# Fourier mixing on one core: where a map quarter's arithmetic and the middle row's products stand

## The chip, the core and the metric

The kernel runs on one core of a Trainium2 chip. Six things work beside each other in that core: TensorE (PE in the rows, with its weight loads as PEld), VectorE (DVE), ScalarE (ACT), GpSimd (POOL), SyncE (SP, which issues most transfers) and the DMA engines. Each engine runs its own instructions in the order in which they stand, and waits where one needs what another engine has not finished. The metric is the device time of one execution in microseconds (us); less is better. The kernel was timed three times, and one execution was profiled.

## What is computed

The program is a trunk of two layers over 512 tokens of width 1024, in float32. The first layer mixes by a state-space scan and neighbourhood attention. The second one, which the change touches, mixes by a two-dimensional Fourier transform and a linear map. Each layer ends in a squared-ReLU MLP.

```python
def fourier_mix(h, w_f):
    hf = jnp.fft.fft2(h.astype(jnp.float32), axes=(1, 2), norm='ortho').real
    return hf.astype(h.dtype) @ w_f
...
        else:
            o = layer // 2
            out_l = fourier_mix(hl, w_fourier[o])
...
        h = h + g1[:, None, :] * rms_norm(out_l, norm_g[layer, 1])
        hf = modulate(rms_norm(h, norm_g[layer, 2]), sh2, sc2)
        h = h + g2[:, None, :] * rms_norm(sqrelu_mlp(hf, w_ff1[layer], w_ff2[layer]), norm_g[layer, 3])
```

## The kernel before

A float32 product is made of three fast ones. An operand is split into a rounded part `hi` (a cast on ACT) and the rest `lo` (a subtraction on DVE): `split_to` (L185). `mm3` (L106 to L108) then multiplies hi by hi, hi by lo and lo by hi. So each operand that is computed on the way costs ACT and DVE work before PE can use it.

The Fourier layer goes in these steps.

* **Stage 1** (L1147) transforms along the tokens and leaves its sums in PSUM tiles `pst`, which are then copied to `xh`, `xl` and `p2`.
* **Features** (the loop over `m_`, L1204 to L1215): for each of four blocks PE makes two products `pa` (L1199 and L1201, plain float32), one 258 and one 256 columns wide. Both are split into `abh` and `abl` (L185), and one column goes to `nyc` (L1210). One more product, `pn`, is split into the small operand `ny`.
* **The map** (`mapw(q)`, L1073) comes in four quarters of 256 output columns. Quarter q is loaded as one tile of 128x2048. On it DVE makes a difference `ws` of its halves (L1081), GpSimd clears a row of `ws`, DVE makes their sum in place (L1084), and both are split: two casts of 128x1024 on ACT and two subtractions of 128x1024 on DVE. A row of 256 elements (`wmid`) is loaded as `w5` and becomes the small operand `wn` (`stack3`, L1060). Quarter 0 (`w0`) is made much earlier, beside the MLP of the layer before. The raw tiles are `wraw82` (quarter 0), the second part of `td` (1), `wraw83` (2) and `w3` (3); the operands of quarters 1 to 3 are `whi44`/`wlo44`, `whi45`/`wlo45` and `whi46`/`wlo46`.
* **The last row** (`last_row(q)`, L1221): four DVE instructions (L1230 once, L1228 three times) that need the sum of quarter q and all four `nyc` columns, and write a quarter of `gn`.
* **Stage 3** (`stage3(q, j)`, L1240): for quarter q and half j of the features PE makes `pq` (12 products), which ACT copies to `qs` (L1256), and `pp` (12 products and one with `ny` and `wn`, L1250). DVE writes their difference to tile 2j of the result `oa` (L1259) and their sum to tile 2j+1 (L1260). For j = 0 there is the middle row: two products into `p2`, of `ny` with `wn` (L1263) and of a column of ones with `gn` (L1264, plain float32), which ACT copies into row 0 of tile 1 (L1265). Before the change this stands at the end of `stage3(q, 0)`.
* **What follows:** when the four quarters of j = 0 are done, tiles 0 and 1 of `oa` go through `residual` (a square with row sums on ACT at L176, `ms` at L178, the root on GpSimd at L180, two DVE passes at L858 and L859) and `normed` (another square over the new `h`, `ms`, a root, one pass `m` at L869). Then `to_cols` transposes both tiles on PE (`ptn`, L888) and splits them into the operand `f1fh`/`f1fl` of the second MLP, whose first products are `pf`. The tiles 2 and 3, from j = 1, follow in the same way.

The order on each engine isn't written out. The program is handed to a scheduler, which lays the instructions out along a modelled timeline; `behind(...)` (L188) tells it to place the instructions inside it only after the ones named. The result is one fixed order for each engine.

Of the kernel before, what the change touches and what calls it, by code (L numbers as in the profile page):

```python
# [93 lines left out]
def trunk(tc, I, out, dump=None):  # L94
# [15 lines left out]
    with es:  # L110
# [24 lines left out]
        def big(tag, dt, nm, n=4096):  # L135
            return bigp.tile([128, n], dt, tag=tag, name=nm)
# [739 lines left out]
        def halves_(t):  # L876
            return [t[:, c * 2052:c * 2052 + 2048] for c in range(2)]
# [172 lines left out]
        def tables():  # L1050
            SY.dma_start(alt, I["alt"])
            SY.dma_start(rev, I["rev"])
            P.memset(zero, 0.0)
            fo["m"] = big("fh", F32, "mf", 4104)
            fo["S"] = W.raw(I["tabS"].rearrange("(k p) n -> p k n", p=128), 4, 514)
            mapw(0, [t.rearrange("p (k n) -> p k n", k=8) for t in halves_(big("fl", F32R, "w0", 4104))])

        wq, plus = {}, {}

# [10 lines left out]
                V.tensor_tensor(f[r:r + 1, 0:n], src, rh.bitcast(F32), SUB)  # L1070
            A.copy(o, f[0:65, 0:n])

        def mapw(q, pair=None, t=None):  # L1073

            cols = slice(q * 256, q * 256 + 256)
            t = W.raw(None, 8, 256) if t is None else t.rearrange("p (k n) -> p k n", k=8)
            wr, wv = t[:, 0:4], t[:, 4:8]
            SY.dma_start(t, I["map"][q].rearrange("p (k n) -> p k n", k=8))
            hi, lo = pair or W.slot(8, 256)
            ws = wide("ws").rearrange("p (k n) -> p k n", k=4)  # L1080
            V.tensor_tensor(ws, wr, wv, SUB)  # L1081
            P.memset(ws[0:1, 0], 0.0)
            split_to(hi[:, 4:8], lo[:, 4:8], ws)
            V.tensor_tensor(wr, wr, wv, ADD)  # L1084
            split_to(hi[:, 0:4], lo[:, 0:4], wr)
            plus[q] = wr
            w5 = small_tile(F32, "w5")[0:1, 0:256]
            SY.dma_start(w5, I["wmid"][:, cols])
            wn = rw.tile([65, 256], F32R, tag="wn", name="wn", bufs=4)
            stack3(w5, wn, (0, 64), (32,))  # L1090
            wq[q] = hi, lo, wn
# [96 lines left out]
        for i in range(2):  # L1188
            evicted = A.copy(PS_[i][:, :, 0:256], ps4[2 + i].rearrange("p (e n) -> p e n", e=2))

        with behind(first, evicted):
            mapw(1, None, spare[:, 2052:4100])
        nyc = rw.tile([128, 4], F32, name="nyc")

        def feat(dst, X, e0, c0, n, row):
# [8 lines left out]
        for m_ in range(4):  # L1204
            ah, al = act_tile("ab")
            even, c = m_ < 2, (m_ % 2) * 128
            pa = ps_mm("pa")[:, 0:258]
            feat(pa, PE_, 0 if even else 2, c if even else 258 + c, 128, even)
            split_to(ah[:, 0:258], al[:, 0:258], pa)
            V.tensor_copy(nyc[:, m_:m_ + 1], pa[:, 0:1])  # L1210
            pa = ps_mm("pa")[:, 0:256]
            feat(pa, PS_, 2 if even else 0, (770 if even else 514) + c, 128, False)
            split_to(ah[:, 258:514], al[:, 258:514], pa)
            AB.append((ah, al))
        pn = ps_mm("pn")[0:1, 0:258]  # L1215
        feat(pn, PE_, 0, 256, 1, True)
        ny = rw.tile([65, 258], F32R, name="ny")
        stack3(pn, ny, (0, 32), (64,))
        mapw(2)
        mapw(3, None, big("fh", F32, "w3", 4104)[:, 0:2048])  # L1220
        gn = wide("gn")  # L1221

        def last_row(q):
# [5 lines left out]
                else:  # L1229
                    V.tensor_scalar(gn[:, cols], plus[q][:, 0], nyc[:, 0:1], None, MULT)  # L1230

        for q in range(4):
            last_row(q)
        SY.dma_start(h[:, 0], hd[0:128])
        SY.dma_start(h[:, 2], hd[128:256])
        for t in range(2):
# [4 lines left out]
        def stage3(q, j):  # L1241
            hi, lo, wn = wq[q]
            cols = slice(q * 256, q * 256 + 256)
            ka = slice(2 + j * 128, 130 + j * 128)
            kb = slice(258 + j * 128, 386 + j * 128)

            def cospart(dst, ks):
                for m_ in range(4):
                    mm3(dst, AB[m_][0][:, ks], AB[m_][1][:, ks], hi[:, m_], lo[:, m_], m_ == 0, False)
                T.matmul(dst, ny[:, ks], wn, start=False, stop=True)  # L1250

            pq = ps_mm("pq")
            for m_ in range(4):
                mm3(pq[:, 0:256], AB[m_][0][:, kb], AB[m_][1][:, kb], hi[:, 4 + m_], lo[:, 4 + m_], m_ == 0, m_ == 3)
            qs = wkp.tile([128, 260], F32, tag="z", name="qs", bufs=3)[:, 0:256]
            A.copy(qs, pq[:, 0:256])  # L1256
            pp = ps_mm("pp")
            cospart(pp[:, 0:256], ka)
            V.scalar_tensor_tensor(oa[:, 2 * j, cols], qs, -1.0, pp[:, 0:256], MULT, ADD)  # L1259
            V.tensor_tensor(oa[:, 2 * j + 1, cols], qs, pp[:, 0:256], ADD)  # L1260
            if j == 0:
                p2 = ps_mm("p2")[0:2, 0:256]
                T.matmul(p2, ny[:, 0:2], wq[q][2], start=True, stop=False)  # L1263
                T.matmul(p2, ones[:, 0:2], gn[:, cols], start=False, stop=True)  # L1264
                A.copy(oa[0:1, 1, cols], p2[0:1])  # L1265

        fh, fl = (halves(big(t, F32R, "f1" + t, 4104)) for t in ("fh", "fl"))
        ns, w1 = {}, {}
        left = [4, 4]
        for q, j in [(0, 0), (1, 0), (2, 0), (3, 0), (0, 1), (1, 1), (2, 1), (3, 1)]:  # L1270
            stage3(q, j)
            left[j] -= 1
            if j == 0 and left[0] == 0:
                for t in range(2):
# [153 lines left out]
```

## Time and profile before

| | |
|---|---|
| three timed runs | 1208.49, 1202.07, 1206.25 us, median 1206.25 |
| the profiled execution | 1203.99 us, of which 1202.2 us are its span (first to last instruction) |
| busy in the span | PE 1153.0 us (96%), DVE 764.3 (64%), ACT 496.9 (41%), POOL 88.4 (7%) |
| granted TensorE clock, mean | 0.985 of full |

The profile shows one execution. Times in its rows count from the start of the span. The Fourier layer's features and stage 3 lie between 782 and 826 us, and the MLP of the second layer from there to the end. Busy shares over the whole span say little of this stretch: PE is the engine that is nearly always busy, but here it is also the one that waits, so the rows below are of this stretch.

### The profile page before, as it was taken

The page shows a single profiled execution, that of the slowest core. Times are in us where ns is not written, and L with a number is a line of the kernel's source. Part 1 is how long each engine was busy: PE and PEld are TensorE (multiplying, and loading weights), DVE is VectorE, ACT ScalarE, POOL GpSimd, SP SyncE. Part 2 cuts the span into 40 slices and gives each one's busy share as a digit, 9 for nine tenths or more (in the row PEclk, how much of TensorE's full clock was granted, in tenths as well). Part 3 has the DMA queues.
Part 4 walks back from the last instruction along what each step waited for, and adds up shares of the span by engine and source line. Part 5 has one row for each costly group of instructions (what it writes and reads, how often), then busy time and mean ns, then how long its engine had stood idle before and what let it go on. Part 6 is the DMA issues. An engine that isn't in the chain of part 4 may idle for free. (4 is left out here: it accounts for less than half of the span.)

```text
span 1202.2 us, 15748 instructions
## 1 busy us (share of the span) xinstructions
PE 1153.0 (96%) x6330; PEld 943.7 (78%) x6330; DVE 764.3 (64%) x1130; ACT 496.9 (41%) x821; POOL 88.4 (7%) x134
## 2 busy tenths in 40 slices
PE   4999999989999999999999999988999999999997
PEld 2687888778977988888888887767988888888886
DVE  7658999666558667667666447787664344344345
ACT  6665446358626643323223133357543223323322
POOL 1001332200002000000000000203000000000001
PEclk8998999989999999999999999998999999999999
DMA  7617444543257375455465422442362332332201
GB/s 269 229 42 209 103 111 132 173 160 102 84 196 261 109 245 194 163 203 180 170 210 168 147 86 72 133 181 77 135 240 76 105 105 71 105 105 75 101 1 71
DMA packets 42368, 168.28 MB, mean 140 GB/s; under 512 B 12587, under 2 KB 14128, under 8 KB 30006
## 3 DMA queue, kind: packets, MB, share of 16 engines
q1 hardware_dynamic: 38726, 155.11, 37.1%
q0 software_dynamic: 2560, 10.42, 3.9%
q10 hardware_dynamic: 1008, 1.72, 0.4%
q8 instruction: 50, 0.82, 0.3%
q14 instruction: 24, 0.20, 0.1%
HBM read 160.49 MB, written 6.75 MB: 139 GB/s over the span
## 5 line engine op out<-in xcount | busy, mean ns | idle before, releaser
L66 ACT CAST whi<-wraw 128x2048 fp32r<-128x2048 f32 (+2 forms) x103 | 147.8, 1459 | 294.0 <-PE pff L108 175.3
L70 DVE TENSOR_TENSOR wlo<-wraw,whi 128x2048 fp32r<-128x2048 f32 (+2 forms) x81 | 161.3, 2000 | 120.5 <-ACT whi L66 120.2
L106 PE MATMUL pff<-whi,ah 128*128 128x512 f32 (+1 forms) x482 | 189.2, 394 | 0.0
L108 PE MATMUL pff<-whi,al 128*128 128x512 f32 (+1 forms) x482 | 189.2, 393 | 0.0
L107 PE MATMUL pff<-wlo,ah 128*128 128x512 f32 (+1 forms) x482 | 188.9, 393 | 0.0
L1000 DVE TENSOR_TENSOR facc<-facc,pff 128x512 f32<-128x512 f32 (+1 forms) x113 | 76.6, 680 | 96.2 <-PE pff L108 96.1
L209 DVE SCALAR_TENSOR_TENSOR gacc<-wraw,cs,gacc 128x1024 f32<-128x1024 f32 x76 | 97.3, 1281 | 24.2 <-DMA wraw<-w_mod 20.8
L107 PE MATMUL pf<-f1fl,whi 128*128 128x512 f32 (+1 forms) x288 | 106.6, 373 | 2.1 <-DVE f1fl L185 1.2
L106 PE MATMUL pf<-f1fh,whi 128*128 128x512 f32 (+1 forms) x288 | 105.7, 374 | 1.9 <-ACT f1fh L185 1.6
L106 PEld LDWEIGHTS pff<-whi,ah 128*128 128x128 f32 x482 | 90.5, 188 | 21.5 <-DVE facc L1000 0.4
L108 PEld LDWEIGHTS pff<-whi,al 128*128 128x128 f32 x482 | 90.5, 188 | 21.3
L107 PEld LDWEIGHTS pff<-wlo,ah 128*128 128x128 f32 x482 | 90.5, 188 | 20.9
L107 PE MATMUL pf<-f0fl,whi 128*128 128x512 f32 (+1 forms) x288 | 105.5, 371 | 1.1 <-DVE f0fl L899 1.1
L108 PE MATMUL pf<-f1fh,wlo 128*128 128x512 f32 (+1 forms) x288 | 105.8, 371 | 0.0
L108 PE MATMUL pf<-f0fh,wlo 128*128 128x512 f32 (+1 forms) x288 | 105.1, 368 | 0.0
L106 PE MATMUL pf<-f0fh,whi 128*128 128x512 f32 (+1 forms) x288 | 103.1, 372 | 1.1 <-ACT f0fh L897 0.7
L984 ACT ACTIVATE rl<-pf 128x512 f32<-128x512 f32 (+1 forms) x72 | 38.9, 547 | 115.8 <-PE pf L108 108.9
L986 DVE TENSOR_TENSOR rl<-rl 128x512 f32<-128x512 f32 (+1 forms) x72 | 44.9, 628 | 60.6 <-ACT ah L985 55.3
L180 POOL TENSOR_TENSOR rstd<-ms,mhalf 128x1 f32<-128x1 f32 x33 | 32.8, 995 | 541.9 <-ACT ms L178 540.3
L107 PEld LDWEIGHTS pf<-f1fl,whi 128*128 128x128 f32 x288 | 54.7, 191 | 12.5 <-DVE f1fl L185 1.6
L106 PEld LDWEIGHTS pf<-f1fh,whi 128*128 128x128 f32 x288 | 54.2, 191 | 12.8 <-ACT f1fh L185 2.1
L108 PEld LDWEIGHTS pf<-f1fh,wlo 128*128 128x128 f32 x288 | 54.8, 191 | 10.1
(459 smaller groups left out, 2170.0 us busy)
## 6 DMA issues: line engine op xcount, KB each, us to landing
wraw<-w_ff SPq DMA_DIRECT2D x64, 1024.0 KB
wraw<-w_mod SPq DMA_DIRECT2D x40, 1024.0 KB
wm<-mod SPq DMA_DIRECT2D x8, 1024.0 KB
wraw<-w_in SPq DMA_DIRECT2D x8, 1024.0 KB
wlo<-w_in POOLq DMA_DIRECT2D x5, 1024.0 KB, 8.5
wraw<-w_out SPq DMA_DIRECT2D x4, 1024.0 KB
M<-kd POOLq DMA_DIRECT2D x32, 64.0 KB, 2.3
G<-norm_g SPq DMA_DIRECT2D x4, 512.0 KB
```

The costliest lines, as they stand in the source:

```text
L66: self.nc.scalar.copy(hi[:, k], t[:, k])
L70: self.nc.vector.tensor_tensor(lo[:, k], t[:, k], hi[:, k].bitcast(F32), SUB)
L106: T.matmul(ps, lh, rh, start=start, stop=False)
L107: T.matmul(ps, lh, rl, start=False, stop=False)
L108: T.matmul(ps, ll, rh, start=False, stop=stop)
L180: P.tensor_tensor(r, ms, mhalf, ALU.pow)
L209: V.scalar_tensor_tensor(acc, w[:, j], cw, acc, MULT, ADD)
L984: A.activation(rl, pf, AF.Relu)
L986: V.tensor_tensor(rl, rl, rl, MULT)
L1000: V.tensor_tensor(dst, dst, pt, ADD)
```

## The change

Five things move; no arithmetic is added or taken away.

1. The loads of the map quarters are taken out of `mapw` into `map_load` and issued ahead of the features.
2. `mapw(1)` and `mapw(2)` stand inside the feature loop, behind the last splits of blocks 2 and 3, where `mapw(1)` stood ahead of the features and `mapw(2)` was free to be placed anywhere.
3. `mapw(3)` stands behind the end of `stage3(0, 0)`.
4. `last_row(1)` stands ahead of stage 3, and `last_row(0)`, `last_row(2)` and `last_row(3)` each behind the end of their own quarter's `stage3(q, 0)`, where all four were free.
5. The middle row's products and copy are taken out of `stage3` into `middle(q)` and follow one quarter later: `middle(0)` after `stage3(1, 0)`, and so on; `middle(2)` and `middle(3)` both after `stage3(3, 0)`.

```diff
         def mapw(q, t, pair=None):
...
-            mapw(1, None, spare[:, 2052:4100])
+            maps[2] = map_load(2)
+            maps[3] = map_load(3, big("fh", F32, "w3", 4104)[:, 0:2048])
...
-            split_to(ah[:, 258:514], al[:, 258:514], pa)
+            split = split_to(ah[:, 258:514], al[:, 258:514], pa)
             AB.append((ah, al))
+            if m_ > 1:
+                with behind(*split):
+                    mapw(m_ - 1, maps[m_ - 1])
...
-        mapw(2)
-        mapw(3, None, big("fh", F32, "w3", 4104)[:, 0:2048])
...
-        for q in range(4):
-            last_row(q)
...
-            if j == 0:
-                p2 = ps_mm("p2")[0:2, 0:256]
-                T.matmul(p2, ny[:, 0:2], wq[q][2], start=True, stop=False)
-                T.matmul(p2, ones[:, 0:2], gn[:, cols], start=False, stop=True)
-                A.copy(oa[0:1, 1, cols], p2[0:1])
+            return V.tensor_tensor(oa[:, 2 * j + 1, cols], qs, pp[:, 0:256], ADD)
...
+        last_row(1)
         for q, j in [(0, 0), (1, 0), (2, 0), (3, 0), (0, 1), (1, 1), (2, 1), (3, 1)]:
-            stage3(q, j)
+            end = stage3(q, j)
+            if j == 0 and q != 1:
+                with behind(end):
+                    last_row(q)
+            if (q, j) == (0, 0):
+                with behind(end):
+                    mapw(3, maps[3])
+            if j == 0 and q:
+                middle(q - 1)
+            if (q, j) == (3, 0):
+                middle(3)
```

The engines' orders differ from the copy of `p2` to the last `pp` of stage 3, and nowhere else; SP's order is the same throughout. Three places follow, with the numbers that the program gives its tiles.

On VectorE, from the copy of `p2` on, before:

```order
L1187 COPY p2_6603<-pst_6527 1x258
L1081 TENSOR_TENSOR ws_6610<-td_6590 128x1024
L1081 TENSOR_TENSOR ws_6701<-wraw83_6697 128x1024
L1084 TENSOR_TENSOR td_6590<-td_6590 128x1024
L1070 TENSOR_TENSOR s3_6621<-w5_6618,rh_6623 1x256
L185 TENSOR_TENSOR abl_6631<-pa_6632,abh_6630 128x258
```

The same place in the changed kernel:

```order
L1190 COPY p2_6603<-pst_6527 1x258
L185 TENSOR_TENSOR abl_6614<-pa_6615,abh_6613 128x258
L1215 COPY nyc_6612<-pa_6615 128x1
L185 TENSOR_TENSOR abl_6614<-pa_6622,abh_6613 128x256
L185 TENSOR_TENSOR abl_6628<-pa_6629,abh_6627 128x258
L1215 COPY nyc_6612<-pa_6629 128x1
L185 TENSOR_TENSOR abl_6628<-pa_6636,abh_6627 128x256
L185 TENSOR_TENSOR abl_6642<-pa_6643,abh_6641 128x258
L1215 COPY nyc_6612<-pa_6643 128x1
L185 TENSOR_TENSOR abl_6642<-pa_6649,abh_6641 128x256
L1084 TENSOR_TENSOR ws_6656<-td_6590 128x1024
```

The splits of the first three feature blocks have moved ahead of the first wide instruction of the map, where three wide ones stood ahead of them.

On VectorE, from the difference of quarter 3's map (`ws`, made of `w3`) to its sum (`w3` in place), before:

```order
L1081 TENSOR_TENSOR ws_6724<-w3_6720 128x1024
L1230 TENSOR_SCALAR gn_6743<-wraw82_6206,nyc_6629 128x256
L185 TENSOR_TENSOR abl_6672<-pa_6673,abh_6671 128x258
L1210 COPY nyc_6629<-pa_6673 128x1
L1230 TENSOR_SCALAR gn_6743<-td_6590,nyc_6629 128x256
L185 TENSOR_TENSOR abl_6672<-pa_6679,abh_6671 128x256
L1230 TENSOR_SCALAR gn_6743<-wraw83_6697,nyc_6629 128x256
L1070 TENSOR_TENSOR s3_6689<-pn_6684,rh_6691 1x258
L1084 TENSOR_TENSOR w3_6720<-w3_6720 128x1024
```

In the changed kernel:

```order
L1263 SCALAR_TENSOR_TENSOR oa_6727<-qs_6747,pp_6749 128x256
L1264 TENSOR_TENSOR oa_6727<-qs_6747,pp_6749 128x256
L1236 TENSOR_SCALAR gn_6722<-wraw82_6205,nyc_6612 128x256
L1084 TENSOR_TENSOR ws_6771<-w3_6610 128x1024
L1070 TENSOR_TENSOR s3_6782<-w5_6779,rh_6784 1x256
L1263 SCALAR_TENSOR_TENSOR oa_6727<-qs_6803,pp_6805 128x256
L1264 TENSOR_TENSOR oa_6727<-qs_6803,pp_6805 128x256
L1234 SCALAR_TENSOR_TENSOR gn_6722<-wraw82_6205,nyc_6612,gn_6722 128x256
L1263 SCALAR_TENSOR_TENSOR oa_6727<-qs_6838,pp_6840 128x256
L1264 TENSOR_TENSOR oa_6727<-qs_6838,pp_6840 128x256
L1236 TENSOR_SCALAR gn_6722<-wraw83_6608,nyc_6612 128x256
L1087 TENSOR_TENSOR w3_6610<-w3_6610 128x1024
```

Quarter 3's difference and sum, which stood among the last feature splits, now stand behind the results `oa` of quarter 0 and of quarters 0 to 2.

On TensorE, around the middle row's last product, that of quarter 3 (`p2_6903` in both), before:

```order
L1250 MATMUL pp_6887<-wn_6734,ny_6688 128x256
L1263 MATMUL p2_6903<-wn_6734,ny_6688 2x256
L1264 MATMUL p2_6903<-gn_6743,ones_85 2x256
L106 MATMUL pq_6941<-w0_6205,abh_6630 128x256
L107 MATMUL pq_6941<-w0_6205,abh_6630 128x256
```

In the changed kernel (`pp_7024` is quarter 2 of j = 1):

```order
L106 MATMUL pp_7024<-whi45_6688,abh_6627 128x256
L107 MATMUL pp_7024<-wlo45_6689,abh_6627 128x256
L108 MATMUL pp_7024<-whi45_6688,abl_6628 128x256
L1270 MATMUL p2_6903<-gn_6722,ones_85 2x256
L106 MATMUL pp_7024<-whi45_6688,abh_6641 128x256
L107 MATMUL pp_7024<-wlo45_6689,abh_6641 128x256
```

The product stood ahead of all of j = 1, and stands now in the middle of the third of its four quarters.

## Rows read from the trace of the kernel before

**Rows 1.** By stretch: length, busy us of PE, PEld, DVE, ACT, POOL; clock, DMA, GB/s
```profile
797.00:800.00 3.00, 3.00 (x16) 3.00 (x16) 2.94 (x9) 1.52 (x4) 0.45 (x1) 0.50 0.00 0
...
807.00:810.00 3.00, 1.85 (x9) 0.44 (x8) 2.94 (x9) 0.87 (x3) 0.00 (x0) 1.00 0.47 126
...
826.00:831.00 5.00, 2.60 (x17) 1.87 (x16) 3.56 (x8) 4.19 (x10) 1.00 (x1) 0.98 0.53 198
831.00:838.00 7.00, 5.57 (x25) 5.17 (x26) 6.95 (x11) 6.52 (x12) 4.37 (x2) 0.53 0.01 2
...
860.00:1000.00 140.00, 140.00 (x621) 113.92 (x620) 73.51 (x74) 48.65 (x56) 0.00 (x0) 1.00 0.37 130
```

**Rows 2.** TensorE in order of time: start, duration, line, operation, [idle before, releaser]
```profile
789.43 1.08 PE L1199 MATMUL pa<-xh,td 128*128 128x258 f32 x4
791.98 1.13 PE L1199 MATMUL pa<-xl,td 128*128 128x256 f32 x4 [1.46 <-DVE abl L185]
794.64 1.03 PE L1199 MATMUL pn<-xh,td 128*1 128x258 f32 x4 [1.54 <-DVE nyc L1210]
...
798.20 0.41 PE L106 MATMUL pp<-w,abh 128*128 128x256 f32 x1
798.41 0.41 PE L107 MATMUL pp<-w,abh 128*128 128x256 f32 x1
...
807.47 1.02 PE L1264 MATMUL p<-gn,ones 128*2 128x256 f32 x4 [0.43 <-DVE gn L1228]
809.21 0.28 PE L1263 MATMUL p<-wn,ny 65*2 65x256 f32 x1 [0.71 <-ACT qs L1256]
...
812.77 0.28 PE L108 MATMUL pp<-whi,abl 128*128 128x256 f32 x1
812.89 0.28 PE L1250 MATMUL pp<-wn,ny 65*128 65x256 f32 x1
...
813.21 0.59 PE L1264 MATMUL p<-gn,ones 128*2 128x256 f32 x2
813.74 0.39 PE L106 MATMUL pq<-w,abh 128*128 128x256 f32 x1
...
826.22 0.87 PE L888 MATMUL ptn<-ident,m 128*128 128x128 f32 x6 [0.18 <-DVE m L869]
```

**Rows 3.** VectorE in order of time, in the same columns
```profile
799.91 1.22 DVE L1084 TENSOR_TENSOR w<-w 128x1024 f32<-128x1024 f32 x1
801.06 0.48 DVE L1228 SCALAR_TENSOR_TENSOR gn<-wraw,nyc,gn 128x256 f32<-128x256 f32 x1
...
808.69 0.48 DVE L1228 SCALAR_TENSOR_TENSOR gn<-w,nyc,gn 128x256 f32<-128x256 f32 x1
809.09 0.41 DVE L1259 SCALAR_TENSOR_TENSOR oa<-qs,pp 128x256 f32<-128x256 f32 x1
809.42 0.41 DVE L1260 TENSOR_TENSOR oa<-qs,pp 128x256 f32<-128x256 f32 x1
...
820.37 1.28 DVE L859 SCALAR_TENSOR_TENSOR h<-oa,rstd,h 128x1024 f32<-128x1024 f32 x1
...
825.42 0.74 DVE L869 TENSOR_SCALAR m<-h,rstd 128x1024 f32<-128x1024 f32 x1
```

**Rows 4.** ScalarE in order of time, in the same columns
```profile
801.95 1.05 ACT L185 CAST whi<-w 128x1024 fp32r<-128x1024 f32 x1
...
814.78 0.35 ACT L1265 COPY oa<-p 1x256 f32<-1x256 f32 x1
815.04 0.29 ACT L178 ACTIVATE ms<-ss,eps 128x1 f32<-128x1 f32 x1
...
815.73 1.06 ACT L176 ACTIVATE sq<-oa 128x1024 bf16<-128x1024 f32 x1
```

**Rows 5.** GpSimd in order of time: the root that ends a row norm
```profile
817.28 1.01 POOL L180 TENSOR_TENSOR rstd<-ms,mhalf 128x1 f32<-128x1 f32 x1 [0.72 <-ACT ms L178]
```

**Rows 6.** SyncE in order of time: loads of the second MLP's weights
```profile
807.44 32.50 SPq L54 DMA_DIRECT2D wraw<-w_ff x4
```

More of the change, by code (lines that the diff above doesn't have):

```diff
@@ L1055, in tables @@
             fo["S"] = W.raw(I["tabS"].rearrange("(k p) n -> p k n", p=128), 4, 514)
-            mapw(0, [t.rearrange("p (k n) -> p k n", k=8) for t in halves_(big("fl", F32R, "w0", 4104))])
+            mapw(0, map_load(0), [t.rearrange("p (k n) -> p k n", k=8) for t in halves_(big("fl", F32R, "w0", 4104))])
         wq, plus = {}, {}
@@ L1071, in stack3, with map_load, mapw @@
             A.copy(o, f[0:65, 0:n])
-        def mapw(q, pair=None, t=None):
+        def map_load(q, t=None):
+            t = W.raw(None, 8, 256) if t is None else t.rearrange("p (k n) -> p k n", k=8)
+            SY.dma_start(t, I["map"][q].rearrange("p (k n) -> p k n", k=8))
+            return t
+        def mapw(q, t, pair=None):
             cols = slice(q * 256, q * 256 + 256)
-            t = W.raw(None, 8, 256) if t is None else t.rearrange("p (k n) -> p k n", k=8)
             wr, wv = t[:, 0:4], t[:, 4:8]
-            SY.dma_start(t, I["map"][q].rearrange("p (k n) -> p k n", k=8))
             hi, lo = pair or W.slot(8, 256)
@@ L1189, in trunk @@
             evicted = A.copy(PS_[i][:, :, 0:256], ps4[2 + i].rearrange("p (e n) -> p e n", e=2))
+        maps = {1: map_load(1, spare[:, 2052:4100])}
         with behind(first, evicted):
-            mapw(1, None, spare[:, 2052:4100])
+            maps[2] = map_load(2)
+            maps[3] = map_load(3, big("fh", F32, "w3", 4104)[:, 0:2048])
         nyc = rw.tile([128, 4], F32, name="nyc")
@@ L1259, in stage3, with middle @@
             V.scalar_tensor_tensor(oa[:, 2 * j, cols], qs, -1.0, pp[:, 0:256], MULT, ADD)
-            V.tensor_tensor(oa[:, 2 * j + 1, cols], qs, pp[:, 0:256], ADD)
-            if j == 0:
-                p2 = ps_mm("p2")[0:2, 0:256]
-                T.matmul(p2, ny[:, 0:2], wq[q][2], start=True, stop=False)
-                T.matmul(p2, ones[:, 0:2], gn[:, cols], start=False, stop=True)
-                A.copy(oa[0:1, 1, cols], p2[0:1])
+            return V.tensor_tensor(oa[:, 2 * j + 1, cols], qs, pp[:, 0:256], ADD)
+        def middle(q):
+            cols = slice(q * 256, q * 256 + 256)
+            p2 = ps_mm("p2")[0:2, 0:256]
+            T.matmul(p2, ny[:, 0:2], wq[q][2], start=True, stop=False)
+            T.matmul(p2, ones[:, 0:2], gn[:, cols], start=False, stop=True)
+            A.copy(oa[0:1, 1, cols], p2[0:1])
         fh, fl = (halves(big(t, F32R, "f1" + t, 4104)) for t in ("fh", "fl"))
```

## The prediction

> **What bounds the kernel now.** I read the busy time by stretch first. From 860 us on TensorE is busy without a gap [rows 1]: 140.00 of 140 us in the row shown. What the Fourier layer loses or gains before that point therefore reaches the end in full, and the question is when the second MLP can begin.
>
> The order of time on TensorE comes next [rows 2]. It shows four waits of PE in the Fourier layer: 1.46 us for an `abl` and 1.54 us for an `nyc` among the features, then 0.43 us for `gn` and 0.71 us for `qs` among the middle row's products. After the first two the granted clock fell: 797 to 800 us stands at 0.50, the lower level of 1.2 GHz [rows 1], and there the products follow each other every 0.21 us (798.20, 798.41), where 0.12 us is the full pace (812.77, 812.89) [rows 2].
>
> The end of the layer is the third thing to see. The transposes start when `m` of tile 1 is there, at 826.22 after 0.18 us of idle [rows 2]. So PE's eight quarters and the row norms of tiles 0 and 1 end together now. The norms begin for tile 1 with a square over the whole of `oa` tile 1 at 815.73 [rows 4]; it needs all four quarters of j = 0 and all four middle rows. From there to the transposes it is 826.22 - 815.73 = 10.5 us, and PE covers that time with j = 1, which began at 813.74 [rows 2]. Whatever makes this square late has no cover left.
>
> **The change, part by part.** I laid the new orders out row by row: an instruction starts when its engine is free and what it waits for is done, with durations and start-to-start distances from the rows.
>
> *Features.* DVE now takes the splits as they come. PE made its first six products without a wait before, the next starting at 789.43 [rows 2]; all eight and `pn` should now run so, and the waits of 1.46 and 1.54 us go. PE reaches stage 3 some 4 us earlier. That is a gain only if what stage 3 needs is earlier too.
>
> *VectorE.* It has the same work, but nearly all of the map now stands behind the third block's splits, at about 789.8 us (product done at 789.43, then a cast and a subtraction of 0.4 us each). Until the sum of quarter 3 it has these to do by the order: 9 wide ones (three differences, two sums, four subtractions of quarters 1 and 2), 1.15 us from start to start (799.91 to 801.06); 4 additions to `gn` at 0.40 (808.69 to 809.09); and 15 others of 256 columns at 0.33 (809.09 to 809.42) [rows 3]. That is 10.35 + 1.6 + 4.95 = 16.9 us, so the sum starts at about 806.6 us, where it started at 799.91 [rows 3]. It takes 1.22, the cast behind it on ACT 1.05 [rows 4]: PE gets the sum's part of quarter 3 at 808.9.
>
> The trace shows the next DVE instruction starting 0.07 us before the end of the one before (799.91 + 1.22 against 801.06) [rows 3]. The Trainium skill (page VectorE: DVE Perf Modes, section The DRAIN you can't avoid) says that the next one does not start until the pipeline is empty; full durations would make the 28 instructions about 2 us longer and the time 2 us more. The rows speak against that, and the sum goes by them.
>
> *TensorE until then.* Quarters 0 to 2 of j = 0 are 75 products at 0.12, 9 us, and PE has them done by about 804.2, with one wait on the way: `ny` is now cast on ACT behind the splits of quarters 1 and 2, at about 800.5, and PE stands some 2.5 us for it. Then it stands for quarter 3 until 808.9, about 4.2 us in two pieces. The 3 us of waits removed in the features come back as 6 to 7 us of new ones.
>
> *The end of j = 0.* From 808.9 PE has, by the order, 38 products at 0.12 and one middle-row product at 0.53 (813.21 to 813.74) [rows 2] up to the last `pp` of quarter 3: 5.1 us, 814.0 (before 812.89).
>
> *The middle row of quarter 3.* `last_row(3)` may start only after quarter 3's results. Its four additions are done on DVE at 818.3, but PE comes to the product behind another middle-row product and 56 products: 814.0 + 0.53 + 56 x 0.12 = 821.2 (before 813.21). With 0.53 for it and 0.35 for the copy (814.78) [rows 4] the square over tile 1 starts at 822.1, against 815.73: 6.4 us later.
>
> *From there to the transposes.* The links are 1.06 for the square, 1.06 for another square that now stands behind it on ACT, 0.29 `ms` [rows 4], 1.01 root [rows 5], 1.28 for `h` [rows 3], 1.06 for the second norm's square, 0.29, 1.01, and 0.74 for `m` [rows 3]: 7.8 us, and about 1.2 of reading the sums, of hand-overs and of standing behind the last results of j = 1 on DVE. Transposes at 822.1 + 9.0 = 831.1, against 826.22: 4.9 us. PE has finished j = 1 by 825.3 and idles nearly 6 us.
>
> *Correction.* The old order, laid out in the same way, puts the square and the transposes 1.2 us before the trace. I add 1.1 to the new one: **6.0 us** later. Ends: 4.9 without it, 6.1 with all of it.
>
> *The clock.* The rows show a fall after 3.0 us of waits within 4.2 us; the wait for quarter 3 is 4.2 us. A stretch like that of 797 to 800 leaves 14 products in 3 us where 25 fit: 11 x 0.12 = **1.3 us**, on the path, since PE runs without a gap from 808.9 to the middle row of quarter 3. The other end is nothing, if the fall lies inside the wait; if the wait for `ny` brings one too, about 1.3 more.
>
> *Nothing for the rest.* SP's order is unchanged. Its loads of `w_ff`, issued from 807.44 on [rows 6], wait for the last reader of quarters 0 and 2's sums and move by a few us; the first of them is used only in the second MLP. `wmid` for quarters 2 and 3 lands while ACT is still at other casts.
>
> Sum: 1203.99 + 6.0 + 1.3 = 1211.3 us for an execution like the profiled one. That one lies 2.3 below the median of the runs, 1206.25, which would give 1213.5. I take **1212.4**, between them; on that scale the kernel before stands at 1205.1.
>
> **The rivals.**
>
> *The clock stays up, or falls where PE stands.* Then it is 6.0 us: 1205.1 + 6.0 = 1211.1. For it: between 807 and 810 PE stood 1.15 of 3 us and the clock stayed at 1.00 [rows 1]. Against it: the new wait is as long as the whole stretch that brought the fall. The Trainium skill (page TensorE: Matmul & The Clock Gate, section HAM oscillation — how this bites in real kernels) has waits between bursts of products put the clock down so that the next burst starts slow. By that rule the 1.3 us are due, and the row of 0.50 agrees; the row of 807 to 810 shows that not every wait does it.
>
> *Part is given back in the norms of tiles 2 and 3.* Between 826 and 838 PE is busy 8.2 of 12 us [rows 1], since ACT and DVE do these norms; if the late start let that stretch close up by half of its 3.8 us of idle and some of its low clock (0.53 in the second row), 3 to 4 us remain: about 1208.5. Against it: the orders put the squares of tiles 2 and 3 behind the first casts after the transposes, as before, so the stretch moves as a whole.
>
> *The front gain reaches the end.* The four waits (1.46, 1.54, 0.43, 0.71) and the low clock (1.3) go, 5.4 us: 1199.7, and faster. It decides at the square over tile 1: only if that starts before 815.73. For it: the features do end 4 us earlier. Against it: quarter 3's sum would have to be made before 800 on a DVE that has 16.9 us of work ahead of it from 789.8. That the change doesn't do what it says is excluded by the orders.
>
> **How the numbers follow.** Forecast (late square, with a fall of the clock) 0.54; no such cost of the clock 0.27; part given back 0.12; faster 0.07. By 0.5% is meant 6 us, about what a measurement of this kernel can tell from no change. The forecast lies beyond it in 0.50 of its 0.54, the second case in 0.12 of 0.27. So slower 0.62, same 0.31, faster 0.07. The range is 1206.5 to 1217.0: it takes in the second case and most of the third, and above it two falls of the clock and a somewhat slower DVE; it leaves out the faster case and the far tails.
>
> **What would show it.** Right: no wait of PE among the features; DVE busy without a gap from 790 to 806 and `w3`'s sum near 806 to 808; PE waits of about 2.5 us for `ny` and 4 us in all before quarter 3's products; the square over tile 1 at 822 to 824; PE idle 5 to 6 us ahead of the transposes of tile 1, near 832 to 834; a stretch at 0.5 between 808 and 815. Wrong: `w3`'s sum before 803, or transposes before 829. If the transposes come at 832 and the end is not 6 us later, the stretch behind them gave it back.

## The result, and the profile after

The changed kernel takes 1215.63 us (median of 17 runs, 1207.85 to 1221.75), the kernel before beside it 1207.86 us (17 runs, 1201.34 to 1214.02). The ratio estimated from all the runs is 1.0072, with an interval of 1.0053 to 1.0091: slower by 8.7 us (the two medians alone differ by 7.8). The forecast was 1212.4, or +7.3, in a range of 1206.5 to 1217.0. Direction and mechanism were right; the sum was too small by 1.4 us against the timed runs and by some 2.3 us against the traces, which follow.

The profiled execution of the changed kernel has a span of 1215.8 us, 13.6 more than that of before. Not all of it is the change. In the two traces the first product of the features and the first product of the second MLP stand here (TensorE in order of time: start, duration, line, operation; the kernel before first):

```profile
782.47 1.14 PE L1199 MATMUL pa<-xh,td 128*128 128x258 f32 x4
...
827.42 0.50 PE L106 MATMUL pf<-f1fh,whi 128*128 128x256 f32 x2 [0.33 <-ACT f1fh L897]
```

and in the changed kernel, with what lies between:

```profile
786.53 1.14 PE L1204 MATMUL pa<-xh,td 128*128 128x258 f32 x4
...
805.99 0.50 PE L1254 MATMUL pp<-wn,ny 65*128 65x256 f32 x2 [2.61 <-ACT ny L1071]
...
814.60 0.58 PE L106 MATMUL pp<-whi,abh 128*128 128x256 f32 x1 [2.54 <-ACT whi L185]
...
815.41 0.41 PE L106 MATMUL pq<-w,abh 128*128 128x256 f32 x1
815.62 0.41 PE L107 MATMUL pq<-w,abh 128*128 128x256 f32 x1
...
822.45 0.28 PE L1254 MATMUL pp<-wn,ny 65*128 65x256 f32 x1
...
830.00 0.59 PE L1270 MATMUL p<-gn,ones 128*2 128x256 f32 x2
...
837.37 0.47 PE L888 MATMUL ptn<-ident,m 128*128 128x128 f32 x2 [2.77 <-DVE m L869]
839.62 1.54 PE L888 MATMUL ptn<-ident,m 128*128 128x128 f32 x6 [1.79 <-DVE m L869]
841.18 0.80 PE L106 MATMUL pf<-f1fh,whi 128*128 128x256 f32 x2
```

The features begin 4.06 us later than before (786.53 against 782.47), although nothing is changed ahead of them: that part differs from one execution to the next (in a second trace of the changed kernel they begin at 785.44). From there on the stage is measured: from the first `pa` to the first `pf` it takes 54.65 us, against 44.95 before, **9.70 us more**. From that `pf` to the end of the span it is 374.62 us, against 374.78: what was lost in the Fourier layer is lost in full, and nothing is given back. To compare a row with those of before, 4.06 is taken off it.

What the change was to remove is gone: PE has no wait among the features, where it had 1.46 and 1.54 us [rows 2]. In its place stand 2.61 us for `ny`, 2.54 us for quarter 3's sum, and 2.77 and 1.79 us ahead of the transposes, where there was 0.18 [rows 2].

VectorE and ScalarE of the changed kernel in order of time:

```profile
794.44 1.22 DVE L1084 TENSOR_TENSOR ws<-td 128x1024 f32<-128x1024 f32 x1
795.68 0.41 DVE L1070 TENSOR_TENSOR s<-w,rh 1x256 f32<-1x256 f32 x1
796.13 0.43 DVE L185 TENSOR_TENSOR abl<-pa,abh 128x258 fp32r<-128x258 f32 x1
...
812.25 1.22 DVE L1087 TENSOR_TENSOR w<-w 128x1024 f32<-128x1024 f32 x1
813.39 0.48 DVE L1234 SCALAR_TENSOR_TENSOR gn<-wraw,nyc,gn 128x256 f32<-128x256 f32 x1
```

```profile
813.50 1.04 ACT L185 CAST whi<-w 128x1024 fp32r<-128x1024 f32 x1 [1.37 <-DVE w L1087]
...
823.56 1.05 ACT L176 ACTIVATE sq<-oa 128x1024 bf16<-128x1024 f32 x1
...
830.63 0.36 ACT L1271 COPY oa<-p 1x256 f32<-1x256 f32 x1 [0.59 <-PE p L1270]
831.02 1.06 ACT L176 ACTIVATE sq<-oa 128x1024 bf16<-128x1024 f32 x1
```

The reader is to see three things. The sum of quarter 3 starts at 812.25 - 4.06 = 808.2, 8.3 us later than before [rows 3]. The square over `oa` tile 1 starts at 831.02 - 4.06 = 827.0, 11.2 us later [rows 4], 7.5 us behind that over tile 0; it stands right behind the copy of the last middle row. And PE starts the last product of quarter 3 (822.45) 7.85 us after its first with the sum (814.60), for work that the forecast put at 5.1.

That last point is the clock. By stretch (length, busy us of PE, PEld, DVE, ACT, POOL; granted clock, DMA share, GB/s):

```profile
808.00:810.00 2.00, 2.00 (x11) 1.91 (x11) 1.97 (x5) 0.37 (x1) 0.15 (x1) 0.50 0.00 0
811.00:814.00 3.00, 1.06 (x5) 0.27 (x3) 3.00 (x7) 1.48 (x3) 0.00 (x0) 0.96 0.00 0
814.00:820.00 6.00, 5.40 (x24) 4.89 (x25) 3.81 (x6) 0.55 (x1) 0.00 (x0) 0.50 0.55 186
820.00:822.00 2.00, 2.00 (x13) 1.31 (x12) 0.00 (x0) 0.96 (x3) 0.00 (x0) 0.86 0.96 369
838.00:842.00 4.00, 2.34 (x8) 1.64 (x8) 1.05 (x2) 1.56 (x4) 0.55 (x1) 0.50 0.00 0
842.00:848.00 6.00, 5.09 (x22) 4.83 (x23) 5.45 (x9) 5.90 (x15) 2.89 (x2) 0.50 0.01 3
860.00:1000.00 140.00, 140.00 (x662) 115.87 (x662) 76.16 (x87) 51.32 (x66) 0.00 (x0) 1.00 0.37 128
```

Behind the wait for `ny` and again behind the wait for quarter 3 the clock stands at 0.50, its lower level of 1.2 GHz, and the products follow each other every 0.21 us (815.41, 815.62). From 860 us on PE is busy without a gap, as before [rows 1].

### The profile page after: what moved, and what is told of

Read it like the earlier page. It is cut to its first block, busy times and chain, and to the rows that moved or that the text cites. A ratio compares the mean times of both kernels' runs of the same rounds, so it can differ in the third digit from the quotient of the medians.

```text
span 1215.8 us, 15745 instructions
## 1 busy us (share of the span) xinstructions
PE 1161.0 (95%) x6330; PEld 950.3 (78%) x6330; DVE 765.3 (63%) x1130; ACT 497.3 (41%) x821; POOL 85.1 (7%) x134
## 3 DMA queue, kind: packets, MB, share of 16 engines
HBM read 160.49 MB, written 6.75 MB: 138 GB/s over the span
```

## The experiments

The theory: the layer ends when the square over tile 1 may start. The change makes that late in two ways, VectorE's sum of quarter 3 and, behind it, the last row of quarter 3, which is pinned behind that quarter's results; the low clock adds to it. The first rival: the late map arithmetic alone sets the end, and the row only stands in its shadow. The second: PE's waits count, each for itself.

The times are ratios to the kernel before, with their intervals. Since the part ahead of the features differs by some microseconds between executions, the traces are compared by the stage, as above; "sum" and "square" are the starts of quarter 3's sum and of the square over tile 1, put on the scale of the trace before. Each column is worked out from rows of the kind shown above; of the kernel before there is one trace.

| | ratio | stage, us against before | sum | square | PE's longest wait in stage 3 |
|---|---|---|---|---|---|
| before | 1 | 0 (44.95) | 799.9 | 815.7 | 0.71 |
| changed | 1.0072 (1.0053 to 1.0091) | +9.70 | 808.2 | 827.0 | 2.61 |
| last rows free | 1.0063 (1.0043 to 1.0083) | +4.78 | 809.9 | 820.8 | 3.01 |
| the same again | 1.0044 (1.0023 to 1.0066) | +4.78 | 809.9 | 820.8 | 3.01 |
| front alone | 1.0021 (1.0002 to 1.0040) | +2.88 | 808.6 | 818.9 | 6.75 |
| back alone | 1.0028 (1.0008 to 1.0048) | +4.82 | 794.9 | 822.5 | 1.07 |
| no middle row of quarter 3 | 1.0027 (1.0009 to 1.0045) | +3.06 | 808.2 | 818.8 | 2.61 |
| changed, again | 1.0095 (1.0070 to 1.0120) | +9.70 | 808.2 | 827.0 | 2.60 |
| wait filled | 1.0073 (1.0045 to 1.0100) | +6.58 | 808.1 | 824.9 | 2.60 |
| `ny` early | 1.0069 (1.0047 to 1.0092) | +9.77 | 808.2 | 827.0 | 2.49 |
| middle rows inline | 1.0066 (1.0038 to 1.0093) | +7.20 | 806.6 | 824.3 | 6.09 |
| row on PE | 0.9984 (0.9966 to 1.0003) | -1.51 | 800.2 | 813.4 | 0.87 |
| row on PE, again | 0.9993 (0.9972 to 1.0014) | -1.51 | 800.1 | 813.4 | 0.87 |

### The last rows free

```diff
             if j == 0 and q != 1:
-                with behind(end):
-                    last_row(q)
+                last_row(q)
```

> The changed kernel with part 4 undone in its pinning: last_row(0), last_row(2) and last_row(3) are free to be placed anywhere instead of behind their quarter's stage3; all else as changed. Theory (the late middle row of quarter 3 sets the end of the layer): the product of quarter 3's middle row then stands ahead of most of j = 1, the square over oa tile 1 starts about 4.5 us earlier than in the changed kernel although the sum of quarter 3 is made 1 to 2 us later, and the time falls by some 3.5 us against the changed kernel, to about 1.004 to 1.005 of the kernel before. Rival (the late map arithmetic sets the end, and the row only stands in its shadow): no less time than the changed kernel, 1.007 or more. Clock alone: no change either, since the wait for quarter 3 stays.

More of the last rows' additions now stand ahead of the sum, which VectorE makes 1.7 us later still; the square comes 6.2 us earlier all the same. TensorE and ScalarE in order of time:

```profile
811.09 0.38 PE L106 MATMUL pp<-whi,abh 128*128 128x256 f32 x1 [1.61 <-ACT whi L185]
...
817.18 0.59 PE L1270 MATMUL p<-gn,ones 128*2 128x256 f32 x2
```

```profile
817.82 1.06 ACT L176 ACTIVATE sq<-oa 128x1024 bf16<-128x1024 f32 x1 [1.76 <-DVE oa L1263]
819.59 1.04 ACT L176 ACTIVATE sq<-oa 128x1024 bf16<-128x1024 f32 x1
```

PE makes the last row's product 6.1 us after quarter 3's first product with the sum, where it took 15.4 in the changed kernel (814.60 to 830.00), and the square over tile 1 follows 1.8 us behind that over tile 0. The stage falls from +9.70 to +4.78 with a later sum: the first rival falls. The ratio of 1.0063 lay above what the stage gives (4.78 us are 0.4%), so the kernel was run again.

> The run with free last rows once more: its time (ratio 1.0063, 1.0043 to 1.0083) stood above what its trace shows in the stage (4.8 us, 1.0040). Theory (the stage is what the orders make it, and the rest is spread of the part ahead of it): the stage is again 4.5 to 5 us longer than before, and the ratio lies nearer 1.004. Rival (something outside the stage costs 3 us): stage 4.8, ratio 1.006 or more again.

The stage came out at +4.78 once more, the ratio at 1.0044, as the theory says. So the first ratio was most likely spread.

### The front alone, and the back alone

The front alone is the changed kernel with the last rows free and the middle rows inside their own stage:

```diff
-                with behind(end):
-                    last_row(q)
+                last_row(q)
...
-            if j == 0 and q:
-                middle(q - 1)
-            if (q, j) == (3, 0):
-                middle(3)
+            if j == 0:
+                middle(q)
```

> Parts 1 to 3 alone: the feature splits first and the map arithmetic behind them as changed, but the last rows free and each middle row inside its own stage3, as before the change. Theory (late middle row): the sum of quarter 3 is as late as in the changed kernel (about 807 to 808 on the scale of the trace before), but the square over tile 1 starts near 816 to 818, and the time is 1 to 3 us over the kernel before (1 from the orders, up to 2 from one fall of the clock after the wait for ny): 1.001 to 1.003. Rival (late map): as slow as the changed kernel, 1.007.

Parts 1 to 3 cost 2.88 us by themselves. The sum is as late as in the changed kernel, yet the square starts at 818.9, 8.1 us earlier than there. The wait on TensorE and a stretch behind it: on PE all the waiting is in one place; the clock falls inside it and is still low for the first products behind it:

```profile
806.79 0.58 PE L1254 MATMUL pp<-wn,ny 65*128 65x256 f32 x1 [6.75 <-ACT ny L1071]
```

```profile
807.20:810.20 3.00, 3.00 (x16) 3.00 (x15) 3.00 (x7) 0.75 (x3) 0.00 (x0) 0.50 0.00 0
```

The back alone takes the map's arithmetic out of the feature loop again. Quarter 3 stands ahead of quarter 2 in its code, though, where it stood behind it before the change:

```diff
+            mapw(1, maps[1])
             maps[2] = map_load(2)
...
-            if m_ > 1:
-                with behind(*split):
-                    mapw(m_ - 1, maps[m_ - 1])
...
         stack3(pn, ny, (0, 32), (64,))
+        mapw(3, maps[3])
+        mapw(2, maps[2])
...
-            if (q, j) == (0, 0):
-                with behind(end):
-                    mapw(3, maps[3])
```

> Parts 4 and 5 alone: last rows behind their quarter, middle rows one quarter later, with the map's arithmetic where it stood before the change. Theory (late middle row): although nothing of the front is moved, the square over oa tile 1 starts about 3 to 4 us later than before, PE stands 2 to 3 us ahead of the transposes, and the time is about 2.5 us over the kernel before: 1.002. Rival (late map): the time of the kernel before, 1.000, or a little less. The two parts' costs (this one and that of the front alone) need not add up to the 8.7 us of the whole.

VectorE, ScalarE (of the kernel before first, then of this run), and the granted clock (the column ahead of the last two):

```profile
796.50 1.22 DVE L1087 TENSOR_TENSOR w<-w 128x1024 f32<-128x1024 f32 x1
```

```profile
813.73 1.06 ACT L176 ACTIVATE sq<-oa 128x1024 bf16<-128x1024 f32 x1 [1.44 <-DVE oa L1259]
```

```profile
813.87 1.06 ACT L176 ACTIVATE sq<-oa 128x1024 bf16<-128x1024 f32 x1 [1.75 <-DVE oa L1263]
824.09 1.06 ACT L176 ACTIVATE sq<-oa 128x1024 bf16<-128x1024 f32 x1
```

```profile
804.00:811.00 7.00, 5.99 (x23) 4.62 (x24) 5.18 (x12) 2.89 (x8) 0.00 (x0) 0.53 0.09 14
```

Here the sum is made 5 us earlier than before the change, and the square over tile 1 still stands 10.2 us behind that over tile 0 and 6.8 us later than before, where I expected 3 to 4. So the pinned row costs time with quarter 3's sum early: +4.82 in the stage, 2.3 us more than expected, and the clock at 0.53 over the `pp` of quarter 2 and the `pq` of quarter 3, after waits of 1.07, 0.92 and 0.39 us, is the likely part above it. The order of the map isn't quite that of before: quarter 2's sum comes 7.4 us later (798.20 - 1.56 = 796.6, against 789.24), and the waits of 1.07 and 0.39 us are for its operands. That isn't what makes the square over tile 1 late, since the one over tile 0 stands at 813.87 - 1.56 = 812.3, 1.4 us earlier than before. The two parts, 2.88 and 4.82, make 7.7 of the 9.7; each has a fall of the clock of its own, so they need not add up.

### Without quarter 3's middle row

```diff
-            if j == 0 and q != 1:
+            if j == 0 and q in (0, 2):
...
-            if (q, j) == (3, 0):
-                middle(3)
```

> The changed kernel without the middle row of quarter 3: last_row(3), middle(3) and its copy are left out, so row 0 of that quarter of tile 1 is not what the layer asks for. All else as changed. Theory (late middle row): the square over tile 1 follows right behind that over tile 0, some 5 to 6 us earlier than in the changed kernel; the transposes then wait for the chain behind tile 0's square, and the time falls by some 4 us against the changed kernel, to 1.003 to 1.004 of the kernel before. What is left over the kernel before is the late sum of quarter 3 and the clock. Rival (late map): 1.007, as changed.

ScalarE in order of time, TensorE's first product with quarter 3's sum and its last of that quarter, and a stretch that holds them:

```profile
816.06 1.05 ACT L176 ACTIVATE sq<-oa 128x1024 bf16<-128x1024 f32 x1
817.44 1.04 ACT L176 ACTIVATE sq<-oa 128x1024 bf16<-128x1024 f32 x1
```

```profile
809.16 0.38 PE L106 MATMUL pp<-whi,abh 128*128 128x256 f32 x1 [2.52 <-ACT whi L185]
...
814.95 0.28 PE L1254 MATMUL pp<-wn,ny 65*128 65x256 f32 x1
```

```profile
808.00:816.00 8.00, 6.84 (x49) 5.66 (x50) 5.02 (x10) 2.26 (x5) 0.00 (x0) 1.00 0.59 204
```

The sum is made at the same place of the stage as in the changed kernel (808.2), the wait for it is the same 2.5 us, and the square comes 8.2 us earlier, more than the 5 to 6 expected. The last row shows what adds to it: here the clock stayed at 1.00 behind the wait. From 809.16 to 814.95 PE makes 43 products and one of a middle row in 5.8 us, where 38 and one took 7.85 us in the changed kernel; without the five more, at 0.12, that is 5.2, so the fall costs 2.7 us up to there. What is left of the stage, +3.06, is the late sum with the clock up.

### The clock

> The changed kernel once more. Its profiled execution had the low clock (0.50) behind the wait for quarter 3, the run without quarter 3's middle row, which has the same orders up to there and the same wait of 2.5 us, did not (1.00). Theory (the waits are fixed, the fall of the clock behind them differs from one execution to the next): the wait for quarter 3 is again 2.5 us in this profile, and the stage from the first feature product to the end of the span is 9.5 us longer than before where the clock falls behind it, about 7.3 where it doesn't. Rival (the fall belongs to the orders): 9.5 us again, with 0.50 behind the wait for quarter 3. Time by ratio: 1.006 to 1.008.

No edit. It came out as the rival said: in this second trace the wait (2.55 us), the fall behind it and the stage (+9.70) are those of the first to 0.1 us. The stretch behind the wait:

```profile
813.00:819.00 6.00, 5.49 (x24) 4.89 (x25) 3.72 (x6) 0.46 (x1) 0.00 (x0) 0.50 0.55 195
```

So the fall came back with the same program. The orders ahead of the wait can't be all that sets it, since the run without quarter 3's row has them too, and there the clock stayed up. Next, PE was given work in that wait (`pq1` is the first product of `pq`).

```diff
...
+            def dummy(dst, n, after):
+                with behind(after):
+                    for _ in range(n):
+                        T.matmul(dst, AB[0][0][:, 2:130], AB[0][0][:, 2:258], start=True, stop=True)
+
             def cospart(dst, ks):
+                late = (q, j) == (3, 0) and 14
+                if late:
+                    dummy(pp[:, 256:512], late, pq1)
...
```

> The changed kernel with 14 products more in the wait for quarter 3: they multiply a block of the features with itself into columns of a PSUM tile that nothing reads, behind the first product of pq for quarter 3. By the orders alone the squares over tile 1 and the transposes come 0.5 to 0.8 us later than in the changed kernel, since the scheduler moves some products of j = 1 ahead. Theory (waits bring the low clock, and it costs about 2 us of the changed kernel's time where it falls on quarter 3): with PE at work there the granted clock stands at 1.00 through quarter 3's products, they follow each other at 0.12 us, and the stage is at or below the better case of the changed kernel, 7 to 8 us over before. Rival (the clock is set by what came before, the wait for ny): a stretch at 0.5 among quarter 3's products all the same, and 8 us or more over before.

TensorE in order of time, then by stretch:

```profile
801.17 0.51 PE L1264 MATMUL pp<-wn,ny 65*128 65x256 f32 x2 [2.60 <-ACT ny L1071]
...
806.85 0.39 PE L106 MATMUL pq<-whi,abh 128*128 128x256 f32 x1 [1.47 <-ACT whi L185]
807.08 1.83 PE L1254 MATMUL pp<-abh 128*128 128x256 f32 x14
```

```profile
801.00:804.00 3.00, 2.83 (x24) 2.77 (x25) 2.90 (x7) 1.77 (x6) 0.00 (x0) 1.00 0.00 0
...
810.00:813.00 3.00, 3.00 (x23) 2.36 (x23) 2.94 (x6) 0.89 (x3) 0.00 (x0) 1.00 0.35 68
```

The first piece of the wait for quarter 3 is there (1.47 us), the second is filled. Quarter 3's products now run at 1.00, and the stage is 3.1 us shorter than the changed kernel's, with 14 products more. The price of the fall is about 3 us, then: 2.7 by the rows of the last section, 3.1 here. The second figure isn't the clock alone, since six more products of j = 1 stand among quarter 3's in this run: the square comes 2.1 us earlier, and the chain from it to the transposes is 1.0 us shorter. The interval of the timed ratio (1.0073) is too wide to show it beside 1.0072 and 1.0095. That the filling keeps the clock up is not shown: the clock stayed up behind the wait for `ny` too, which isn't filled and has the same length and the same orders ahead of it as in the changed kernel, where it fell; and it stayed up without any filling behind the same wait for quarter 3 in the run without that quarter's row.

The last run on the waits takes the one for `ny` away, by making `pn` and `ny` ahead of quarter 2's arithmetic:

```diff
+            if m_ == 3:
+                pn = ps_mm("pn")[0:1, 0:258]
+                feat(pn, PE_, 0, 256, 1, True)
+                ny = rw.tile([65, 258], F32R, name="ny")
+                stack3(pn, ny, (0, 32), (64,))
             if m_ > 1:
                 with behind(*split):
                     mapw(m_ - 1, maps[m_ - 1])
-        pn = ps_mm("pn")[0:1, 0:258]
-        feat(pn, PE_, 0, 256, 1, True)
-        ny = rw.tile([65, 258], F32R, name="ny")
-        stack3(pn, ny, (0, 32), (64,))
```

> The changed kernel with pn and the operand ny made ahead of the arithmetic of quarter 2, in the feature loop; all else as changed. The wait of 2.6 us for ny goes, and three short ones for quarter 2's operands (0.3 to 0.8 us) come. Theory (PE has slack until quarter 3, whose sum VectorE makes at the same time as before): quarter 3's products start when they did, PE stands 4 to 5 us in two pieces ahead of them, the square over tile 1 is where it was, and the time is that of the changed kernel to 0.5 us, plus or minus one fall of the clock (2 us). Rival (each us of PE's waits counts): 2.5 us less than the changed kernel.

TensorE's two waits for quarter 3:

```profile
806.71 0.38 PE L106 MATMUL pq<-whi,abh 128*128 128x256 f32 x1 [2.33 <-ACT whi L185]
809.59 0.58 PE L106 MATMUL pp<-whi,abh 128*128 128x256 f32 x1 [2.49 <-ACT whi L185]
```

The wait of 2.6 us is gone and +9.77 remains: PE now stands 2.33 + 2.49 us for quarter 3, whose sum comes when it did. The second rival falls. A wait of PE ahead of something that is late anyway costs nothing here, and neither does the fall of the clock behind the wait for `ny`, which is gone as well.

### The middle rows inline, the pins kept

```diff
-            if j == 0 and q:
-                middle(q - 1)
-            if (q, j) == (3, 0):
-                middle(3)
+            if j == 0:
+                middle(q)
```

> The changed kernel with part 5 undone: each middle row stands inside its own quarter's stage3 again, the last rows stay pinned behind their quarter's results. Theory (the pin of last_row(3), not the move of the products, makes the row late): by the orders the sum of quarter 3 is made 1.6 us earlier than in the changed kernel, PE has all of quarter 3's products done some 2 us earlier, and still comes to the last row's product behind most of j = 1, so that the square over tile 1 starts only 0.6 us earlier; the stage is 5.5 us over before by the orders, up to 8 with a fall of the clock: 1.005 to 1.007. Rival (the move of the products to one quarter later is at fault): the square follows quarter 3's results as in the front alone, 1.002 to 1.003.

The middle rows' products of quarters 2 and 3 on TensorE, and the two squares on ScalarE:

```profile
812.38 0.59 PE L1270 MATMUL p<-gn,ones 128*2 128x256 f32 x2
819.36 0.59 PE L1270 MATMUL p<-gn,ones 128*2 128x256 f32 x2
```

```profile
811.36 1.06 ACT L176 ACTIVATE sq<-oa 128x1024 bf16<-128x1024 f32 x1 [1.78 <-DVE oa L1263]
820.38 1.06 ACT L176 ACTIVATE sq<-oa 128x1024 bf16<-128x1024 f32 x1
```

Though quarter 3's row stands inside its own stage in the code, its product comes 7.0 us after that of quarter 2, and the square 9.0 us behind the one over tile 0. It is the pin that makes the row late, not the move of the products by a quarter: in the code this run differs from the front alone in the pins of the last rows only, and the stage is 7.20 against 2.88, 4.3 us. In both the clock falls in a wait of 6 to 7 us for `ny`. Against the changed kernel it saves 2.5 us: the sum is 1.6 us earlier, and no second fall lies on quarter 3. The square is 2.6 us earlier than there, where I expected 0.6.

### The middle row on TensorE

From these a version follows that has nothing pinned behind results. The middle row is made from the features' first columns and the quarter's operands on PE, `last_row` is no longer called and nothing is written to `gn`, `ny` is made first of the features, and quarters 2 and 3 both stand behind block 3's splits.

```diff
+        pn = ps_mm("pn")[0:1, 0:258]
+        feat(pn, PE_, 0, 256, 1, True)
+        ny = rw.tile([65, 258], F32R, name="ny")
+        stack3(pn, ny, (0, 32), (64,))
         AB = []
...
                     mapw(m_ - 1, maps[m_ - 1])
+                    if m_ == 3:
+                        mapw(3, maps[3])
...
-            T.matmul(p2, ones[:, 0:2], gn[:, cols], start=False, stop=True)
+            hi, lo, _ = wq[q]
+            for m_ in range(4):
+                mm3(p2, AB[m_][0][:, 0:2], AB[m_][1][:, 0:2], hi[:, m_], lo[:, m_], False, m_ == 3)
...
```

> A version made from the theory. The middle row is made on PE from the features' first columns and the quarter's operands (12 products of 2 columns' results by 256, in place of the four DVE additions to gn and the product with ones), each inside its own quarter as before the change, so nothing stands behind VectorE's results; last_row and gn are gone; ny is made first of the features; the feature splits come first, and quarters 2 and 3 follow behind block 3's splits. PE has some 3.6 us more of products, DVE 16 instructions (6 us) less. Theory (VectorE's queue and the late row set the end): the sum of quarter 3 is made near 799 to 800, PE has no wait of over 1 us in stage 3, the square over tile 1 starts near 813, and the end is about 1 us earlier than before the change by the orders, up to 2.5 with the clock up: 0.998 to 0.999. Rival (the layer ends when PE's products end, so work added to PE adds to the time): 1.002 to 1.003.

The square over tile 1 on ScalarE, and one stretch from the end of the features to the transposes:

```profile
810.05 1.04 ACT L176 ACTIVATE sq<-oa 128x1024 bf16<-128x1024 f32 x1
```

```profile
790.00:821.00 31.00, 28.84 (x239) 26.28 (x238) 26.69 (x36) 20.78 (x43) 4.79 (x6) 1.00 0.12 39
```

The sum starts where it did before the change (table), the square 2.3 us earlier, PE has no wait above 0.87 us, and the clock stays at 1.00 through the stage.

> The version with the middle row on PE once more, to narrow its interval (0.9984, 0.9966 to 1.0003). By its trace the stage is 2.2 us shorter than before the change: 0.998 in the ratio. If it is no gain at all, 1.000 or more.

Both traces have the stage 1.51 us shorter than before, from the first `pa` to the first `pf`; the 2.2 us expected counts to the end of the span, where the two traces give 2.16 and 1.25. The ratios, 0.9984 and 0.9993, have intervals that reach over 1. It is faster than the changed kernel, since its intervals and those of 1.0072 and 1.0095 lie well apart; against the kernel before it is a gain in the trace that the timed runs don't settle.

## Why the prediction was right, and where its sum was off

*Features.* Right: six products without a wait before, eight and `pn` now.

*VectorE's sum of quarter 3: mis-sized by 1.6 us.* Forecast 806.6, measured 808.2, and PE got it at 810.5 (814.60 - 4.06) instead of 808.9. The instructions counted were the right ones, but the first of them began at 790.4, not 789.8, and they took 17.8 us (794.44 to 812.25), not 16.9. Nearly all of that is the four subtractions of one row, which I had put among those at 0.33 us from start to start: they take 0.45 (795.68 to 796.13), and the instruction of 128x1024 ahead of each takes 1.24 to its start (794.44 to 795.68) instead of 1.14 (812.25 to 813.39). The short overlap of one VectorE instruction with the next, for which I had left out 2 us of waiting, is seen again: 812.25 + 1.22 against 813.39. It is absent on both sides of a subtraction of one row (794.44 + 1.22 against 795.68, 795.68 + 0.41 against 796.13). The prediction took only one half from the Trainium skill (page VectorE: DVE Perf Modes, section The DRAIN you can't avoid): behind the sentence on the empty pipeline, that section says that a next op that is not held starts earlier. The trace has both kinds, the first beside the subtractions of one row only.

*TensorE's waits.* 2.5 us for `ny` was forecast and 2.61 measured. For quarter 3 I had 4.2 us in two pieces and there is one of 2.54: the low clock behind `ny` stretched quarter 2's products over the first piece. The run with `ny` early has both pieces.

*The late row: right, and 0.5 us too short.* I had 7.2 us from the last product of quarter 3 to that row's product, and 0.9 from there to the square; measured 7.5 (822.45 to 830.00) and 1.0. Both are too small, by 0.5 us together. That the pin makes the row late, and that the row binds, is shown three times: freed, the stage loses 4.9 us although the sum is later; left out, 6.6 us, of which some 3 are the clock that stayed up; with quarter 3's sum early, the pinned rows cost 4.8, a fall of the clock included.

*The clock: mis-sized by 1.4 us.* I put one fall at 1.3 us, from the 3 us at 0.50 in the kernel before. On quarter 3 it lasted from about 813.8 (the row of 811 to 814 at 0.96) to about 820.6 (that of 820 to 822 at 0.86), all but its first 0.8 us on the path: 7.85 us up to the last product of quarter 3 instead of 5.1, so 2.7. The wait for `ny` brought a fall of its own, off the path. The sentence I took from the Trainium skill (page TensorE: Matmul & The Clock Gate, section HAM oscillation — how this bites in real kernels), that waits between bursts make the next burst start slow, agrees with that trace, and the runs do not make it a rule: behind waits of 2.5 us the clock was at 0.50 in the changed kernel and at 1.00 without quarter 3's row.

*From the square to the transposes: too long by 1.5 us.* I had 9.0 and a correction of 1.1, since the old order, laid out in the same way, came out short. Measured are 8.6 (831.02 to 839.62). The correction did not carry over.

So 7.3 + 1.6 + 1.4 + 0.5 - 1.5 = 9.3, and the transposes of tile 1 do come 9.3 us later (839.62 - 4.06 = 835.6, against 826.22 [rows 2]); the stage is 9.7 us longer and the span, from the first `pa` to its end, 9.5 (429.27 us against 419.73). That the forecast came as near as it did is in part luck: the terms that were too small, 3.5 us in all, met one that was too large by 1.5. The signs named ahead show the same: the sum lies within its band (808.2), while the square (827.0, not 822 to 824) and the transposes (835.6, not 832 to 834) lie behind theirs, and PE stood 4.6 us ahead of them, not 5 to 6. By the runs, taken in this order, the 9.7 us of the stage are some 3.1 for the late sum of quarter 3 (what is left without the row and with the clock up on quarter 3), 3.5 for the row (up to the filled wait) and 3.1 for the fall of the clock. The shares are rough, since the orders of these runs differ in more than the part that each stands for.

*The rivals.* The clock that stays up would have given 6.0; the filled wait, where it does, shows 6.6 in the stage. A loss given back in the norms of tiles 2 and 3 is ruled out: from the first `pf` to the end it is 374.1 to 375.5 us in all thirteen traces. The front gain that reaches the end would have needed a square before 815.73; it needs another program, the one with the row on PE, where it starts at 813.4.

## What to carry to other kernels

Before taking waits off an engine, ask which instruction the end hangs on and what the move puts ahead of it: here 3 us of waits were traded for an operand made 8 us later. A pin behind results also pins all that follows from them; the smallest operation of the stage, four additions and one row, cost about as much as the late sum of quarter 3 (3.5 and 3.1 us by the split above), since 56 products stood ahead of it. A wait had a second price where the clock fell behind it, and that price was paid only where the products behind it were on the path: some 3 us on quarter 3, nothing behind `ny`.

## What was not expected of the hardware

* The time ahead of the stage, where the orders are the same, differs between traces by up to 8 us (the first `pa` stands between 778.5 and 786.7 in the thirteen), and between two traces of one kernel by up to 3.3 (781.27 and 784.59 with the last rows free), while the stage repeats to 0.1 us in the three kernels that were traced twice. For half a per cent in one stage, the trace of one execution told more here than ten timed ones.
* The low clock came back in the same place in both traces of the changed kernel (814.60 and 813.51 are the same product), and yet the same wait of 2.6 us for `ny`, with the same orders ahead of it, brought a fall in the changed kernel and none in the run with the filled wait. In the same way the wait of 2.5 us for quarter 3 brought a fall in the changed kernel and none in the run without that quarter's row. What sets them apart is open.
* Behind the transposes the clock stood at 0.50 from 838 to 848 us and beyond in the changed kernel, and for about 7 us before [rows 1], and the time from `pf` to the end was the same to 0.2 us. Between 842 and 848 us ACT is busy 5.90 of 6 us and DVE 5.45, so it is likely that they set the pace there.
